# A decoder trunk on one core: the accumulators of the feed-forward block products in PSUM tiles of one bank each, and the last slab's sum in the other PSUM pool

## The chip, the cores and the metric

The kernel runs on one core of a Trainium2 chip. The metric is the device time of one execution in microseconds (us). The engines are called by the profile's names: PE is TensorE (PEld its weight loads), ACT is ScalarE, DVE is VectorE, POOL is GpSimd, SP is SyncE, which here only issues DMAs. L1395 is line 1395 of the kernel.

## The reference

One inference step of one decoder layer for 512 prompt tokens and 64 sample tokens of width 1024, in float32: a gated convolution and a gated linear recurrence side by side, a cross-attention into 256 memory tokens, and a SwiGLU feed-forward block. Only the last matters here:

```
xn = rms_norm(x, g[4])
gate, up = jnp.split(xn @ w_ffn_in, 2, axis=-1)         # 1024 -> 2 x 2816
x = x + rms_norm((jax.nn.silu(gate) * up) @ w_ffn_out, g[5])   # 2816 -> 1024
```

## The kernel before

**Products in three parts.** Every float32 matrix product is made of three matmuls on operands split into a high and a low part (high by high, high by low, low by high). The features lie on the 128 partitions and the 576 tokens (64 sample, 512 prompt) in the free dimension. A weight block is loaded to a raw tile by SP, ACT casts it to the high part (`whi`, L102) and DVE subtracts that from the raw tile to get the low part (`wlo`, L103). There are five raw buffers, four `whi` and four `wlo` buffers; blocks are prepared three ahead of their use.

**PSUM.** There are two pools of PSUM tiles. `mm` has two buffers of two banks each (`[128, 2, 512]` float32, made by `mmt`), `aux` has four buffers of one bank each (`[128, 512]`, made by `auxt`). A buffer is handed out again once all who used it are done; the tile framework adds every wait.

**The feed-forward block.** The 2816 hidden features are 22 slabs of 128. Slabs 0 to 6 are computed plainly. Slabs 7 to 21 are computed in 15 calls of `ffn_pair` (L1399): the gate and the up product of one slab, for the left and the right half of the tokens (288 each), come from seven block products instead of eight, with combinations of inputs and of weights in the manner of Strassen. Each product (`product`, L1389) is 12 matmuls of 288 columns, four blocks of features by three parts, into one accumulator. In their order the seven write accumulators 0, 1, 0, 2, 0, 1, 0. Accumulators 0 and 1 are the two banks of one `mm` tile, accumulator 2 is an `aux` tile; the three are taken at the start of the slab (`begin`, L1401). Accumulator 0 is not cleared between its four products, nor accumulator 1 between its two: a later product adds to the earlier ones. After each product one read takes what has been summed so far:

- first product, accumulator 0: `p1` (L1407), a copy on ACT; second, accumulator 1: `p5` (L1410), a copy on ACT;
- third, accumulator 0: `p6` (L1413), a copy on ACT; fourth, accumulator 2: `p2` (L1416), an add on DVE;
- fifth, accumulator 0: `p7` (L1419), on DVE; sixth, accumulator 1: `p3` (L1423), on DVE, then a silu on ACT (L1426);
- seventh, accumulator 0: `p4` (L1432, L1433), two multiplications on DVE, then the split of the result on ACT and DVE (L102, L103).

**The order.** From here on the order of PE, ACT and DVE is the order of the program (a manual schedule). A step of `run_steps` (L257) issues the product's matmuls, then the read of its accumulator, then half of a weight block's preparation (`w_part`, L191: one cast on ACT and one subtraction on DVE), then what is marked as late. One weight block of two products is 2 x 256 KB.

The 15 slabs come in two parts, of 7 and 8. After the first part the eight output slabs of the second linear layer add 7 slabs' contribution (`ffo_part`, L1532, one `mm` tile each). After the second part they add the last 8 slabs' contribution (`ffo`, L1559, one `mm` tile each), for output slabs 3 to 7 in two token groups of 320 and 256, the 320 group of all of them first.

**The last slab.** `last` (L1655) is the last step: output slab 7 for the group of 256 tokens. It sums in an `aux` tile, `ps`, 12 matmuls of half the product; then come the transposes of slab 6 (`tok_out`, L1592, an `aux` tile, copied out by ACT at L1599), three blocks of transposed output of the 320 group (`out_a` by `by_token`, L1463, an `aux` tile each, copied out by ACT at L1473 and sent by DMA), the column sums of squares (`sums_of`, L1602, an `aux` tile, L1606), the second 12 matmuls, and the norm, the transposes into `p2`, and the output. Three `out_a` blocks of the other half of the features are issued just before `last`.

Of the kernel before, what the change touches and what calls it, by code (L numbers as in the profile page):

```python
# [20 lines left out]
HN = T // 2  # L21
# [31 lines left out]
def decoder_step(  # L53
# [22 lines left out]
    def new(dt=F32, n=1):  # L76
        if n > 1:
            return [new(dt) for _ in range(n)]
        i = free_units.popleft()
        t = upool.tile([128, UNIT], dt, tag=f"u{i}", name=f"u{i}")  # L80
        owner[id(t)] = (i, t)
        return t

    def free(*ts):
        for t in ts:
            if isinstance(t, (list, tuple)):
                free(*t)
            else:
                i, _ = owner.pop(id(t))
                free_units.append(i)  # L90

    def mmt():
        return mm_p.tile([128, 2, 512], F32, tag="mm", name="mm")

    def auxt():
        return aux_p.tile([128, 512], F32, tag="aux", name="aux")
# [13 lines left out]
    def hs(h):  # L110
        return slice(HS[h], HS[h] + HW[h])
# [16 lines left out]
    def gemm(out, W, X, h, k0=0, nk=KT, first=True, last=True):  # L128
        wh, wl = W
        for k in range(nk):  # L130
            xh, xl = X(k0 + k, h)
            mm3(out, wh[:, k, :], wl[:, k, :], xh, xl, first and k == 0, last and k == nk - 1)
# [173 lines left out]
    def gain(v, k):  # L306
        return gT[:, v * 8 + k:v * 8 + k + 1]
# [1047 lines left out]
    def gg_split(j, cs, t):  # L1355
        if gg_h[j] is None:
            gg_h[j], gg_l[j] = new(F32R), new(F32R)
        split(gg_h[j][:, cs], gg_l[j][:, cs], t[:, cs])
# [28 lines left out]
    FF = {}  # L1387

    def product(W, b, ps, X, xs, first, last):  # L1389

        wh, wl = W
        xh, xl, o = X
        for i in range(4):
            k, x = 4 * b + i, 2 * i + o
            PE.matmul(ps, lhsT=wh[:, k, :], rhs=xh[x][:, xs], start=first and i == 0, stop=False, skip_group_check=True)  # L1395
            PE.matmul(ps, lhsT=wh[:, k, :], rhs=xl[x][:, xs], start=False, stop=False, skip_group_check=True)  # L1396
            PE.matmul(ps, lhsT=wl[:, k, :], rhs=xh[x][:, xs], start=False, stop=last and i == 3, skip_group_check=True)  # L1397

    def ffn_pair(j):  # L1399

        def begin():  # L1401
            ps = mmt()
            FF["b"] = ps[:, 0, :HN], ps[:, 1, :HN], auxt()[:, :HN]
            FF["t"], FF["u"] = new(), new()

        def p1():
            ACT.copy(FF["t"][:, L], FF["b"][0])  # L1407

        def p5():
            ACT.copy(FF["u"][:, L], FF["b"][1])  # L1410

        def p6():
            ACT.copy(FF["t"][:, R], FF["b"][0])  # L1413

        def p2():
            DVE.tensor_add(FF["t"][:, L], FF["t"][:, L], FF["b"][2])  # L1416

        def p7():
            DVE.scalar_tensor_tensor(FF["u"][:, L], FF["b"][0], -1.0, FF["u"][:, L], op0=ALU.mult, op1=ALU.subtract)  # L1419

        def p3():
            t = FF["t"]
            DVE.tensor_add(t[:, R], t[:, R], FF["b"][1])  # L1423

        def p3_late():
            ACT.activation(FF["t"][:, 0:T], FF["t"][:, 0:T], AF.Silu)  # L1426
            if j == KF - 1:
                free(x3n_h, x3n_l, t_h[0::2], t_l[0::2])

        def p4():  # L1430
            t, u = FF["t"], FF.pop("u")
            DVE.scalar_tensor_tensor(t[:, L], FF["b"][0], -1.0, t[:, L], op0=ALU.mult, op1=ALU.mult)  # L1432
            DVE.tensor_mul(t[:, R], t[:, R], u[:, L])  # L1433
            free(u)

        def p4_late():
            t = FF.pop("t")
            if j == KF - 1:
                free(t_h[1::2], t_l[1::2])
            gg_split(j, slice(0, T), t)  # L1440
            free(t)

        N, TT = (x3n_h, x3n_l), (t_h, t_l)
        return [("EG", (*N, 0), L, 0, True, True, (p1, None), begin), ("s1", (*TT, 0), L, 1, True, True, (p5, None), None),
                ("s2", (*TT, 1), R, 0, False, True, (p6, None), None), ("OG", (*N, 1), L, 2, True, True, (p2, None), None),
                ("s3", (*TT, 0), R, 0, False, True, (p7, None), None), ("s4", (*N, 1), R, 1, False, True, (p3, p3_late), None),
                ("OU", (*TT, 1), L, 0, False, True, (p4, p4_late), None)]

    def ffn_pairs(js):
        todo = [(j, p) for j in js for p in ffn_pair(j)]  # L1450
        for n in range(0, len(todo), 2):
            two = todo[n:n + 2]
            w = w_blocks([block(p[0], j) for j, p in two])
            for b, (j, (_, X, xs, bank, first, last, post, begin)) in enumerate(two):
                def pe(W=None, b=b, X=X, xs=xs, bank=bank, first=first, last=last, begin=begin):
                    if W is not None:
                        FF["W"] = W
                    if begin:
                        begin()
                    product(FF["W"], b, FF["b"][bank], X, xs, first, last)  # L1460
                step([w] if b == 0 else [], pe, post, prep="pair")
# [90 lines left out]
    def acc_add():  # L1552

        if "sq" in F:
            sq, s = F.pop("sq")
            DVE.tensor_add(F["acc"][:, s], F["acc"][:, s], sq[:, s])
            free(sq)
# [34 lines left out]
    def tok_out(n):  # L1592
        fg = F.pop(("fg", n))
        cs = slice((n % 4) * 128, (n % 4 + 1) * 128)
        ps = auxt()
        for i in range(2):
            PE.transpose(ps[:, i * 128:(i + 1) * 128], fg[:, i * 128:(i + 1) * 128], ident)
        for i in range(2):
            ACT.copy(ft[i][n // 4][:, cs], ps[:, i * 128:(i + 1) * 128])  # L1599
        free(fg)  # L1600

    def sums_of(cols):  # L1602

        ps = auxt()
        for i, src in enumerate(cols):
            PE.matmul(ps[:, i:i + 1], lhsT=src, rhs=ones_f[:, 0:1], start=True, stop=True)  # L1606
        return ps

    def rstd_from(o, m):

        v, y, q = (rs[:, o + k * m:o + (k + 1) * m] for k in range(3))
        ACT.activation(y, v, AF.Ln, scale=1.0 / D)
        ACT.activation(y, y, AF.Exp, scale=-0.5)
        DVE.tensor_mul(q, y, y)
        DVE.scalar_tensor_tensor(q, q, -0.5 / D, v, op0=ALU.mult, op1=ALU.mult)
        DVE.scalar_tensor_tensor(y, q, 1.5, y, op0=ALU.add, op1=ALU.mult)
        return y

    def finish(i, r):
        c0, m = htiles[1][i]  # L1620
        for d in range(2):
            t = ft[i][d]
            DVE.scalar_tensor_tensor(t[:, 0:512], t[:, 0:512], r, x2t[i][d][:, 0:512], op0=ALU.mult, op1=ALU.add)
            (nc.sync if i % 2 else nc.scalar).dma_start(
                out=tok_rows(y_sample, y_prompt, c0, m)[:, d * 512:(d + 1) * 512], in_=t[:, 0:512])
# [14 lines left out]
    def out_a(i, c4):  # L1640
        def go():
            c0, m = htiles[0][i]
            by_token(fA, 0, i, c4, nc.sync if i % 2 else nc.scalar, tok_rows(y_sample, y_prompt, c0, m))
        return go
# [10 lines left out]
    def last(W):  # L1655

        k0, nk = kgroups[2]
        ps, p2 = auxt(), auxt()
        gemm(ps[:, 0:256], W, G, 1, k0, 4, True, False)
        acc_add()  # L1660
        tok_out(6)
        for i in range(3):
            out_a(i, 1)()
        p0 = sums_of([F["acc"][:, c0:c0 + m] for c0, m in htiles[1]])
        gemm(ps[:, 0:256], [w[:, 4:, :] for w in W], G, 1, k0 + 4, 4, False, True)
        DVE.tensor_scalar(rs[:, 16:18], p0[:, 0:2], D * EPS, None, op0=ALU.add)
        fg, f1 = new(), fs[7][:, hs(1)]
        DVE.tensor_add(f1, f1, ps[:, 0:256])
        ACT.activation(fg[:, 320:576], f1, AF.Square)
        DVE.tensor_scalar(fg[:, 0:256], f1, gain(5, 7), None, op0=ALU.mult)  # L1670
        p1 = sums_of([fg[:, 320:448], fg[:, 448:576]])
        for i in range(2):
            PE.transpose(p2[:, i * 128:i * 128 + 128], fg[:, i * 128:i * 128 + 128], ident)
        DVE.tensor_add(rs[:, 20:22], rs[:, 16:18], p1[:, 0:2])
        r = rstd_from(20, 2)
        for i in range(2):
            ACT.copy(ft[i][1][:, 384:512], p2[:, i * 128:i * 128 + 128])
        for i in range(2):
            finish(i, r[:, i:i + 1])
# [64 lines left out]
```

## Time and profile before

| | |
|---|---|
| three runs | 1205.54, 1206.62, 1207.12 us; median 1206.62 |
| profiled execution | 1205.55 us, its span 1203.7 us |
| granted clock of PE, mean | 0.998 of full |
| busy share of the span | PE 96%, PEld 93%, DVE 56%, ACT 50%, POOL 12% |
| slabs 7 to 13 in `ffn_pair` | 877.8 to 977.6 us of the span |
| slabs 14 to 21 in `ffn_pair` | 1022.5 to 1136.7 us |
| HBM | 184 GB/s over the span |

The profile is one execution. Busy times add up the recorded durations of an engine's instructions. Matmuls are pipelined: one is recorded as taking 0.29 us while the next starts 0.13 us later, so the distance between starts tells what a matmul costs. Idle time before a group of instructions is given with the instruction that ended most of it.

### The profile page before, as it was taken

How to read it: one execution, taken by the hardware profiler on the slowest of the kernel's cores; microseconds unless marked ns; L12 is line 12 of the kernel's file. 1: busy time of each engine (PE TensorE's matmuls, PEld its weight loads, DVE VectorE, ACT ScalarE, POOL GpSimd, SP SyncE). 2: the span in 40 equal slices, each digit the busy share in tenths (PEclk: the TensorE clock that was granted, in tenths of full speed). 3: DMA queues.
4: the chain of work that ended last, by engine and by line, in shares of the span. 5: the costliest groups of instructions: out<-in, count | busy, mean ns of one | idle time of the engine just before them, and what ended most of it. 6: DMA issues, size and time to landing. Idle time of an engine off the chain costs nothing.

```text
span 1203.7 us, 21042 instructions
## 1 busy us (share of the span) xinstructions
PE 1150.5 (96%) x8524; PEld 1116.2 (93%) x8524; DVE 675.0 (56%) x1082; ACT 603.1 (50%) x1030; POOL 147.4 (12%) x301
## 2 busy tenths in 40 slices
PE   6999999999999999999999999999988899888896
PEld 5999999999999999999988999999987789777896
DVE  6666556642233346897677779883144543554445
ACT  5656556642122246665567777853344421444443
POOL 5433333112011010222100000000000000000000
PEclk9999999999999999999999999999999999999999
DMA  8556777467457455666755855653444433444602
GB/s 231 167 180 175 181 175 207 146 143 188 153 140 176 121 164 152 195 199 202 229 184 206 268 166 162 195 172 111 122 120 128 124 99 101 123 129 135 197 6 79
DMA packets 256859, 191.13 MB, mean 159 GB/s; under 512 B 9432, under 2 KB 241896, under 8 KB 256634
## 3 DMA queue, kind: packets, MB, share of 16 engines
q1 hardware_dynamic: 249812, 149.95, 41.8%
q0 software_dynamic: 6144, 38.50, 12.5%
q8 instruction: 67, 1.10, 0.4%
q10 hardware_dynamic: 806, 1.34, 0.3%
q14 instruction: 30, 0.25, 0.1%
HBM read 180.36 MB, written 40.85 MB: 184 GB/s over the span
## 4 chain that ended last, share of the span: by engine, by line
PE 90%; DVE 4%; ACT 3%; issue 1%; DMA 1%; POOL 0%; SPq 0%; DVEq 0%; ACTq 0%
PE mm L107 22%; PE mm L108 22%; PE mm L106 22%; PE mm L1395 5%; PE mm L1397 3%; PE mm L1396 3%; PE aux L1225 1%; PE aux L1209 1%; PE aux L106 1%; PE aux L107 1%; PE aux L108 1%; ACT u L102 1%; PE aux L1397 1%; PE aux L1396 1%; PE aux L1395 1%
## 5 line engine op out<-in xcount | busy, mean ns | idle before, releaser
L106 PE MATMUL mm<-u,whi 128*128 128x288 f32 (+2 forms) x2024 | 602.4, 298 | 0.3 <-ACT u L458 0.3
L108 PE MATMUL mm<-u,wlo 128*128 128x288 f32 (+2 forms) x2024 | 599.2, 296 | 0.5 <-POOL wlo L431 0.5
L107 PE MATMUL mm<-u,whi 128*128 128x288 f32 (+2 forms) x2024 | 598.7, 296 | 0.5 <-DVE u L103 0.5
L103 DVE TENSOR_TENSOR wlo<-wraw,whi 128x1024 fp32r<-128x1024 f32 (+2 forms) x294 | 303.9, 1035 | 238.8 <-ACT whi L102 230.1
L102 ACT CAST whi<-wraw 128x1024 fp32r<-128x1024 f32 (+2 forms) x294 | 261.0, 898 | 286.5 <-PE mm L107 217.7
L107 PEld LDWEIGHTS mm<-u,whi 128*128 128x128 f32 x2024 | 382.6, 189 | 2.1 <-DVE u L103 1.3
L106 PEld LDWEIGHTS mm<-u,whi 128*128 128x128 f32 x2024 | 382.6, 189 | 1.9 <-ACT u L458 0.9
L108 PEld LDWEIGHTS mm<-u,wlo 128*128 128x128 f32 x2024 | 382.3, 189 | 1.1 <-POOL wlo L431 0.9
L1395 PE MATMUL mm<-u,whi 128*128 128x288 f32 x360 | 112.4, 312 | 31.1 <-DVE u L1419 8.3
L1395 PEld LDWEIGHTS mm<-u,whi 128*128 128x128 f32 x360 | 67.5, 187 | 45.0 <-DVE u L1423 11.7
L1396 PE MATMUL mm<-u,whi 128*128 128x288 f32 x360 | 106.1, 295 | 0.0
L1397 PE MATMUL mm<-u,wlo 128*128 128x288 f32 x360 | 106.0, 294 | 0.0
L102 ACT CAST u<-u 128x576 fp32r<-128x576 f32 (+6 forms) x117 | 58.9, 532 | 90.8 <-DVE u L640 26.2
L103 DVE TENSOR_TENSOR u<-u,u 128x576 fp32r<-128x576 f32 (+6 forms) x117 | 65.4, 578 | 16.9 <-ACT u L102 16.7
L1397 PEld LDWEIGHTS mm<-u,wlo 128*128 128x128 f32 x360 | 67.6, 188 | 0.0
L1396 PEld LDWEIGHTS mm<-u,whi 128*128 128x128 f32 x360 | 67.6, 188 | 0.0
L103 DVE TENSOR_TENSOR u<-aux,u 128x512 fp32r<-128x512 f32 (+2 forms) x60 | 32.8, 584 | 3.6 <-ACT u L102 3.5
L1426 ACT ACTIVATE u<-u 128x576 f32<-128x576 f32 x15 | 10.3, 685 | 45.1 <-DVE u L1423 45.1
L102 ACT CAST u<-aux 128x512 fp32r<-128x512 f32 (+2 forms) x60 | 27.9, 514 | 6.7 <-DVE u L103 2.1
L106 PE MATMUL aux<-u,u 128*128 128x256 f32 (+1 forms) x96 | 27.8, 294 | 0.0
L107 PE MATMUL aux<-u,u 128*128 128x256 f32 (+1 forms) x96 | 27.6, 289 | 0.0
L108 PE MATMUL aux<-u,u 128*128 128x256 f32 (+1 forms) x96 | 27.6, 288 | 0.0
(290 smaller groups left out, 1204.6 us busy)
## 6 DMA issues: line engine op xcount, KB each, us to landing
wraw<-in_w_in_dram SPq DMA_DIRECT2D x48, 512.0 KB, 4.2
sum_s<-in_w_ffn_in_dram POOLq DMA_DIRECT2D x24, 960.0 KB, 8.2
wraw<-sum_s SPq DMA_DIRECT2D x60, 256.0 KB, 3.3
wraw<-in_w_ffn_in_dram SPq DMA_DIRECT2D x28, 512.0 KB, 3.7
wraw<-in_w_ffn_in_dram SPq DMA_DIRECT2D x45, 256.0 KB, 3.3
wraw<-in_w_mix_out_dram SPq DMA_DIRECT2D x16, 512.0 KB, 3.9
wraw<-in_w_kv_x_dram SPq DMA_DIRECT2D x16, 512.0 KB, 3.8
wraw<-in_w_q_x_dram SPq DMA_DIRECT2D x16, 512.0 KB, 3.7
```

What stands on the lines that cost most here:

```text
L102: ACT.copy(hi, src)
L103: DVE.tensor_sub(lo, src, f(hi))
L106: PE.matmul(out, lhsT=wh, rhs=xh, start=start, stop=False)
L107: PE.matmul(out, lhsT=wh, rhs=xl, start=False, stop=False)
L108: PE.matmul(out, lhsT=wl, rhs=xh, start=False, stop=stop)
L1209: PE.transpose(ps[:, d * 256 + i * 128:d * 256 + (i + 1) * 128], kr[i][:, h * 256 + d * 128:h * 256 + (d + 1) * 128], ident)
L1225: PE.matmul(ps[0:m], lhsT=t[:, k * 64:k * 64 + m], rhs=src, **kw)
L1395: PE.matmul(ps, lhsT=wh[:, k, :], rhs=xh[x][:, xs], start=first and i == 0, stop=False, skip_group_check=True)
L1396: PE.matmul(ps, lhsT=wh[:, k, :], rhs=xl[x][:, xs], start=False, stop=False, skip_group_check=True)
L1397: PE.matmul(ps, lhsT=wl[:, k, :], rhs=xh[x][:, xs], start=False, stop=last and i == 3, skip_group_check=True)
L1426: ACT.activation(FF["t"][:, 0:T], FF["t"][:, 0:T], AF.Silu)
```

## The change

The first two accumulators of `ffn_pair` become `aux` tiles of one bank each and the third becomes one bank of an `mm` tile. In `last` the sum moves from an `aux` tile to one bank of an `mm` tile, and the `aux` tile `p2` is taken later, behind the second sums of squares. No instruction is added or removed.

```diff
     def ffn_pair(j):
 
         def begin():
-            ps = mmt()
-            FF["b"] = ps[:, 0, :HN], ps[:, 1, :HN], auxt()[:, :HN]
+            FF["b"] = auxt()[:, :HN], auxt()[:, :HN], mmt()[:, 0, :HN]
             FF["t"], FF["u"] = new(), new()
...
     def last(W):
 
         k0, nk = kgroups[2]
-        ps, p2 = auxt(), auxt()
+        ps = mmt()[:, 0, :]
         gemm(ps[:, 0:256], W, G, 1, k0, 4, True, False)
...
-        p1 = sums_of([fg[:, 320:448], fg[:, 448:576]])
+        p1, p2 = sums_of([fg[:, 320:448], fg[:, 448:576]]), auxt()
```

## Rows read from the trace of the kernel before

**Rows 1.** the page: busy time, share of the span and instructions of each engine

```profile
PE 1150.5 (96%) x8524; PEld 1116.2 (93%) x8524; DVE 675.0 (56%) x1082; ACT 603.1 (50%) x1030; POOL 147.4 (12%) x301
```

**Rows 2.** page, line 1395 on PE: busy, mean ns, idle before, releaser

```profile
L1395 PE MATMUL mm<-u,whi 128*128 128x288 f32 x360 | 112.4, 312 | 31.1 <-DVE u L1419 8.3
```

**Rows 3.** line 1395: idle before it until the named instruction, us and times

```profile
...
  DVE u L1419: 20.0, 30
...
  ACT u L1410: 18.1, 30
...
```

**Rows 4.** timeline, products A to F of one pair: start, us, engine, line

```profile
907.75 0.29 PE L1397 MATMUL mm<-u,wlo 128*128 128x288 f32 x1
...
908.08 0.40 ACT L1407 COPY u<-mm 128x288 f32<-128x288 f32 x1
...
908.53 0.40 PE L1395 MATMUL mm<-u,whi 128*128 128x288 f32 x1 [0.49 <-ACT u L1407]
...
908.77 0.30 PE L1396 MATMUL mm<-u,whi 128*128 128x288 f32 x1
...
911.11 0.30 PE L1396 MATMUL mm<-u,whi 128*128 128x288 f32 x1
...
915.63 0.29 PE L1397 MATMUL mm<-u,wlo 128*128 128x288 f32 x1
915.96 0.46 DVE L1419 SCALAR_TENSOR_TENSOR u<-mm,u 128x288 f32<-128x288 f32 x1 [0.54 <-PE mm L1397]
...
916.71 0.30 PE L1396 MATMUL mm<-u,whi 128*128 128x288 f32 x1
```

**Rows 5.** chain that ended last, in order of time: start, us, engine, line

```profile
1060.72 0.47 DVE u L1419
...
1132.06 0.47 DVE u L1419
```

**Rows 6.** timeline of the same pair: reads of one tile beside writes of another

```profile
906.56 0.29 PE L1397 MATMUL mm<-u,wlo 128*128 128x288 f32 x1
906.57 0.46 DVE L1432 SCALAR_TENSOR_TENSOR u<-mm,u 128x288 f32<-128x288 f32 x1 [1.40 <-PE mm L1397]
...
912.78 0.40 ACT L1413 COPY u<-mm 128x288 f32<-128x288 f32 x1 [1.45 <-PE mm L1397]
...
914.16 0.29 PE L1395 MATMUL mm<-u,whi 128*128 128x288 f32 x1
...
918.86 0.69 ACT L1426 ACTIVATE u<-u 128x576 f32<-128x576 f32 x1 [3.49 <-DVE u L1423]
```

**Rows 7.** stretches: us, busy PE, PEld, DVE, ACT, POOL, granted clock, DMA share, GB/s

```profile
905.00:962.00 57.00, 48.70 (x338) 44.99 (x337) 29.36 (x53) 24.76 (x49) 0.00 (x0) 1.00 0.43 124
700.00:760.00 60.00, 59.96 (x452) 58.94 (x451) 52.15 (x88) 45.77 (x82) 1.62 (x3) 1.00 0.59 172
1196.00:1204.00 8.00, 0.68 (x6) 0.44 (x5) 3.38 (x8) 0.73 (x4) 0.00 (x0) 0.69 0.36 134
```

**Rows 8.** SP's waits in 880 to 1136 us; the page's DMA issues

```profile
SPq L185 <- DVE wlo L103: 169.0, 53, 5.4
...
wraw<-sum_s SPq DMA_DIRECT2D x60, 256.0 KB, 3.3
```

**Rows 9.** timeline of the last slab: start, us, engine, line

```profile
1189.17 0.39 PE L106 MATMUL aux<-u,whi 128*128 128x256 f32 x1 [0.92 <-ACT u L1599]
...
1190.21 1.07 ACT L1473 COPY u<-aux 128x512 f32<-128x512 f32 x2 [0.62 <-ACT u L1473]
1190.22 0.28 PE L108 MATMUL aux<-u,wlo 128*128 128x256 f32 x1
...
1191.73 0.43 ACT L1599 COPY u<-aux 128x128 f32<-128x128 f32 x2 [0.45 <-PE aux L1470]
...
1192.22 0.66 PE L1470 MATMUL aux<-ident,u 128*128 128x128 f32 x4 [0.23 <-ACT u L1599]
...
1192.71 0.58 PE L1606 MATMUL aux<-ones_f,u 128*128 128x1 f32 x4
```

## The prediction, made before the changed kernel was run

> **What bounds the kernel now.** I began with the page's busy shares: TensorE (PE) is busy in 96% of the span, VectorE (DVE) in 56%, ScalarE (ACT) in 50% [rows 1]. So only what PE does, or waits for, can move the time. Next come the page's groups of instructions. Nearly all of PE's lines have under 1 us of idle time before them; line 1395, the first matmul in each step of a block product, has 31.1 us, and no other line that the change touches comes near it [rows 2]. The view of that single line names the four instructions it waits for: the reads of an accumulator at lines 1407, 1410, 1419 and 1423, each 30 times (15 pairs, once on PE and once on its weight load); two of the four rows are shown, the other two read the same [rows 3].
>
> The timeline says why. Call the seven products of a pair A to G in their order: A, C, E, G write bank 0 of the `mm` tile, B and F write its bank 1, D writes the `aux` tile. A's last matmul starts at 907.75, p1 (line 1407) copies bank 0 from 908.08 for 0.40 us, and B, which writes bank 1, starts only at 908.53, when that copy is over [rows 4]. B needs nothing from the copy: its bank is another. So the wait is kept by tile and not by bank. C waits in the same way for p5's read of B's bank, F for p7's read of bank 0, G for p3's read of bank 1. At the borders where the neighbour lies in another tile nothing waits: A runs on while p4 still reads the pair before in the other `mm` buffer (906.56 beside 906.57), and E, which really needs p6's copy of bank 0 (912.78, 0.40 us), starts at 914.16 without a wait, because D stood between [rows 6].
>
> **The change, part by part.**
>
> *Removed: four waits per pair.* I measure them between starts. From the second matmul of C (911.11) to the last of E (915.63) are 34 steps without a wait: 4.52 / 34 = 0.1329 us each. From A's last matmul to B's second are 908.77 - 907.75 = 1.02 us where two steps would take 0.27: 0.75 lost; from E's last to F's second 916.71 - 915.63 = 1.08: 0.81 lost [rows 4]. With the equal ones at C and G that is 2 x 0.75 + 2 x 0.81 = 3.12 us per pair. A check by the period: the chain passes line 1419 at 1060.72 and, five pairs later, at 1132.06, so a pair takes 71.34 / 5 = 14.27 us [rows 5]; its 84 matmuls need 84 x 0.1329 = 11.16; the rest is 3.11. Over 15 pairs: 15 x 3.12 = **46.8 us**.
>
> The idle column would give less: 31.1 us [rows 2], and a sum of 1174. The two differ because a matmul is booked busy for 0.29 to 0.40 us while the next one starts 0.13 later. The Trainium skill, Trainium Kernel Development and Optimization, section Performance Expectations, says that matmul busy time is a bad metric because matmuls are pipelined; by that rule the starts are to be taken, and the trace agrees (a row of 0.29 us repeats every 0.133). I take 46.8 and leave 31.1 out of the range, since the period confirms the former.
>
> *Left in their place: the true waits.* After the change bank 0 and bank 1 are `aux` tiles of their own and the third accumulator is an `mm` tile. A write then waits only for the last read of its own bank, which always has one product or more in between: C for p1 across B, E for p6 across D, F for p5 across three products, G for p7 across F. C's first matmul is due 13 steps, 1.73 us, after A's last; p1 ends 0.33 + 0.40 = 0.73 us after it [rows 4], so 1.0 us is spare. G after p7: 0.33 + 0.46 = 0.79 against 1.73. E after p6 has that same form today and shows no wait [rows 6]. Cost: zero; if DVE or ACT were late by over 0.9 us it would come back. Behind p3 stands the silu, which must be done before p4: it runs 918.86 to 919.55 [rows 6], F's last matmul is at 916.71 + 10 x 0.133 = 918.04, so it ends 1.51 us after that one; p4 is due 1.59 + 0.33 = 1.92 after it. Covered, by 0.4 us, and nothing on PE waits for p4 in the next pair.
>
> *Moved: buffers.* `aux` has four buffers and a pair now takes two, so pairs alternate as they do on two `mm` buffers today. The third accumulator takes one `mm` buffer, freed after D. No instruction or DMA is added. The kind of tile does not change a matmul's duration: products into `aux` today keep the same step, D being inside the 34 steps above.
>
> *The other engines in a shorter pair.* The stretch 905 to 962 holds four periods: DVE 29.36 / 4 = 7.3 us per pair, ACT 24.76 / 4 = 6.2, both below 11.16. Weights: 7 blocks of 256 KB per pair are 1.835 MB; in 11.16 us that is 164 GB/s, against 124 now. The stretch 700 to 760 moved 172 GB/s with PE busy for 59.96 of its 60 us [rows 7]. SP, which issues these loads, mostly waits for a raw buffer to come free (169.0 us) and not for data, and a load lands 3.3 us after its issue [rows 8]; five raw buffers hold five times two products, some 16 us of work. Cost: zero.
>
> *The last slab.* Its accumulator leaves the `aux` ring. Today its first matmul waits 0.92 us for the copy at line 1599 to free a buffer. It loses that wait, but ACT's chain of copies and output issues sets the pace here: the fourth block of transposes waits for the copy at 1191.73 to 1192.16, and the column sums (line 1606) come only after it, 1192.71 [rows 9]. With one `aux` buffer more, those transposes go ahead of that copy, and the sums follow it directly: 1192.71 - 1192.22 = 0.49 us earlier, and with them the second half of the slab and the tail. Bounds: 0, if ACT is the whole bound, and 0.92, the whole first wait; I take **0.5**, the piece that stands on the chain.
>
> **Sum:** the profiled execution, 1205.55 us, less 46.8 and 0.5, gives 1158.3. The median shown is 1206.62, 1.07 above it; the same offset gives **1159 us**. Taking the step as 0.132 instead moves it by 1 us, the bounds of the tail by 0.5: alone this case lies in 1157 to 1162.
>
> **Rivals.**
>
> 1. *One wait per pair takes the place of the four.* If the ring handed A of the next pair the `aux` buffer that p4 still reads, A would wait as F does now, 0.81 us, in the 13 pairs that follow a pair: 10.5 us, 1169.5. Against it: A does not wait today on two buffers, and the first matmul of the last slab waited for the oldest buffer's copy, not the newest [rows 6, 9]. Chance 0.07.
> 2. *Supply catches PE.* If the loads only came half-way, 144 GB/s, a pair would take 1.835 MB / 144 = 12.74 us, 1.58 more than 11.16: 24 us back, 1183. For it: the stage's blocks come on one queue. Against: 172 GB/s elsewhere, and SP's waits [rows 7, 8]. Chance 0.05.
> 3. *Nothing changes.* The dependence could go by pool or by engine rather than by tile. Then 1206, or 0.5 less with the tail. Against it: the last slab's matmuls write an `aux` buffer (1190.22) while ACT reads other `aux` buffers (1190.21, for 1.07 us) [rows 9]. The Trainium skill, Perfetto Trace Analysis, section Optimization Strategy, reads a gap that repeats as a possible sign that there is no room to allocate the next tile; by that rule a change that adds no buffer would leave the gaps, and the time, as they are. The trace disagrees: A and D, the writers into new buffers, do not wait, while B, C, F and G write into buffers held since the pair began. Chance 0.05.
> 4. *Slower: PE runs the prepared weights dry, stands in lumps, and its clock falls.* Place: the pair stage, beyond rival 2. The clock does drop in this kernel: 0.69 on average in the last 8 us, where PE had 0.68 us of work, and 1.00 in the pair stage with its stops of under 1 us [rows 7]. At the lower level a product takes 12 x 0.133 = 1.6 us more. With rival 2's 1.58 us lost, 1.54 of the 3.12 is left, so one such product per pair decides; two make 15 x (1.58 + 3.2 - 3.12) = 25 us, 1231. Against it is all that speaks against rival 2. Chance 0.03.
>
> **How the numbers follow.** The forecast has 0.80. Its range with the working of both bounds is 1157 to 1162; I stretch it to 1156 and, to take in rival 1, to 1171. A measurement of this kernel can tell about 0.2% (2.4 us) from no change. Faster: forecast and rivals 1 and 2, 0.92; same: rival 3, 0.05; slower: rival 4, 0.03.
>
> **What would show it.** Right: line 1395 with next to no idle time on PE, 11.2 us between pairs, about 160 GB/s in the stage, clock 1.00, the sums of the last slab directly behind the copy at 1599. Wrong: line 1395 waiting for 1432 (rival 1), PE or DVE waiting for the raw weights (rival 2), the same four releasers as now (rival 3), a clock under 1.00 in the pair stage (rival 4).

## The result, and the profile after the change

The changed kernel takes 1158.35 us (median; 1157.59 to 1158.93) where the kernel before took 1206.08 us beside it. The ratio is 0.9603, with a 95% interval of 0.9587 to 0.9620. The forecast was 1159, the range 1156 to 1171.

The profiled execution took 1157.59 us, its span is 1155.8 us, 47.9 less than before, with the same mean clock of 0.998. The page's busy shares and its group for line 1395, which answer to [rows 1] and [rows 2]:

```profile
PE 1134.3 (98%) x8524; PEld 1113.9 (96%) x8524; DVE 675.0 (58%) x1082; ACT 603.2 (52%) x1030; POOL 146.9 (13%) x301
...
L1395 PE MATMUL aux<-u,whi 128*128 128x288 f32 x360 | 105.9, 294 | 0.0
```

DVE and ACT do the same work as before to 0.1 us. Line 1395 has no idle time left, against 31.1 us. PE's busy time *fell*, by 16.2 us, though it executes the same matmuls. The page's busy time of an engine counts time in which matmuls overlap only once; 8524 matmuls of 0.29 us, added up, would be more than twice the span. (The busy time of a group, as in the second line, is the sum of its durations.) Before the change the first matmul after each of the 60 stops lay alone for 0.24 us until the next one began (908.53 to 908.77 in [rows 4]) instead of 0.13, and the last one before the stop lay alone for all of its 0.29 us instead of 0.13: (0.11 + 0.16) x 60 = 16.2. Idle time and this time together, 31.1 + 16.2 = 47.3, are what starts against starts had shown.

The changed file is one line shorter behind the edit, so that p1 is now L1406, p5 L1409, p6 L1412, p2 L1415, p7 L1418, p3 L1422, the silu L1425 and p4 L1431. The timeline of the end of A, the start of B, and the end of E up to p4 in one pair, answering to [rows 4] (start, us, engine, line):

```profile
901.23 0.29 PE L1397 MATMUL aux<-u,wlo 128*128 128x288 f32 x1
...
901.36 0.30 PE L1395 MATMUL aux<-u,whi 128*128 128x288 f32 x1
...
901.56 0.40 ACT L1406 COPY u<-aux 128x288 f32<-128x288 f32 x1
...
907.59 0.30 PE L1397 MATMUL aux<-u,wlo 128*128 128x288 f32 x1
907.72 0.29 PE L1395 MATMUL aux<-u,whi 128*128 128x288 f32 x1
...
907.92 0.46 DVE L1418 SCALAR_TENSOR_TENSOR u<-aux,u 128x288 f32<-128x288 f32 x1 [0.55 <-PE aux L1397]
...
909.19 0.30 PE L1397 MATMUL aux<-u,wlo 128*128 128x288 f32 x1
909.33 0.29 PE L1395 MATMUL aux<-u,whi 128*128 128x288 f32 x1
...
910.01 0.69 ACT L1425 ACTIVATE u<-u 128x576 f32<-128x576 f32 x1 [2.68 <-DVE u L1422]
...
910.77 0.29 PE L1397 MATMUL aux<-u,wlo 128*128 128x288 f32 x1
...
911.17 0.46 DVE L1431 SCALAR_TENSOR_TENSOR u<-aux,u 128x288 f32<-128x288 f32 x1 [0.59 <-PE aux L1397]
```

B starts 0.13 us after A's last matmul and runs while p1 copies accumulator 0 (901.56 to 901.96). F starts 0.13 us after E's last matmul and overlaps p7, and G follows F without a step missed, 1.74 us after E's last matmul; p7 had ended at 908.38. The period, from p4 to p4 four pairs later, answering to [rows 5]:

```profile
900.05 0.46 DVE L1431 SCALAR_TENSOR_TENSOR u<-aux,u 128x288 f32<-128x288 f32 x1 [0.59 <-PE aux L1397]
...
944.53 0.46 DVE L1431 SCALAR_TENSOR_TENSOR u<-aux,u 128x288 f32<-128x288 f32 x1 [0.59 <-PE aux L1397]
```

44.48 / 4 = 11.12 us a pair, against 14.27; over 84 matmuls that is 0.1324 us each, no step lost. Busy time of four periods, answering to [rows 7] (columns as there):

```profile
905.00:949.50 44.50, 44.50 (x338) 44.50 (x337) 28.76 (x51) 24.33 (x48) 0.00 (x0) 1.00 0.54 157
```

And SP's waits in 880 to 1090 us, answering to [rows 8] (us in total, times, longest):

```profile
SPq L185 <- DVE wlo L103: 136.3, 53, 5.4
```

PE is busy for the whole stretch, at clock 1.00, with loads of 157 GB/s. SP still spends 136.3 us waiting for raw buffers to come free, and PE waits for no load.

The last slab, answering to [rows 9]. The last addition of the residual before the change (line 1636 there, 1635 now):

```profile
1188.72 0.83 DVE L1636 TENSOR_TENSOR u<-u,u 128x640 f32<-128x640 f32 x1
```

And the slab after the change:

```profile
1140.60 0.36 PE L106 MATMUL mm<-u,whi 128*128 128x256 f32 x1
...
1141.31 0.83 DVE L1635 TENSOR_TENSOR u<-u,u 128x640 f32<-128x640 f32 x1
...
1144.33 0.43 ACT L1598 COPY u<-aux 128x128 f32<-128x128 f32 x2 [0.45 <-PE aux L1469]
...
1144.81 0.61 PE L1605 MATMUL aux<-ones_f,u 128*128 128x1 f32 x4 [0.23 <-ACT u L1598]
```

The first matmul waits for nothing (0.92 us before). The column sums stand directly behind ACT's copy, 3.50 us after the last addition of the residual began on DVE (L1635); before the change the same distance was 3.99 (1188.72 to 1192.71): 0.49 gained.

### The profile page after: what moved, and what is told of

Its sections match the earlier page's. It is cut to its first block, busy times and chain, and to the rows that moved or that the text cites. A ratio compares the mean times of both kernels' runs of the same rounds, so it can differ in the third digit from the quotient of the medians.

```text
span 1155.8 us, 21040 instructions
## 1 busy us (share of the span) xinstructions
PE 1134.3 (98%) x8524; PEld 1113.9 (96%) x8524; DVE 675.0 (58%) x1082; ACT 603.2 (52%) x1030; POOL 146.9 (13%) x301
## 4 chain that ended last, share of the span: by engine, by line
PE 94%; DVE 2%; ACT 1%; DMA 1%; issue 1%; POOL 0%; SPq 0%; DVEq 0%; ACTq 0%
PE mm L107 23%; PE mm L108 23%; PE mm L106 23%; PE aux L1397 4%; PE aux L1396 4%; PE aux L1395 4%; PE aux L1225 1%; PE aux L1209 1%; PE aux L106 1%; PE aux L107 1%; PE aux L108 1%; PE mm L1397 1%; PE mm L1396 1%; PE mm L1395 1%; DMA wraw<-in_w_in_dram 1%
## 5 line engine op out<-in xcount | busy, mean ns | idle before, releaser
L107 PEld LDWEIGHTS mm<-u,whi 128*128 128x128 f32 x2032 | 384.5, 189 | 2.4 <-DVE u L103 1.3
L106 PEld LDWEIGHTS mm<-u,whi 128*128 128x128 f32 x2032 | 384.3, 189 | 2.2 <-ACT u L458 1.2
L108 PEld LDWEIGHTS mm<-u,wlo 128*128 128x128 f32 x2032 | 384.0, 189 | 0.8 <-POOL wlo L431 0.6
L1397 PE MATMUL aux<-u,wlo 128*128 128x288 f32 x360 | 106.2, 295 | 0.0
L1396 PE MATMUL aux<-u,whi 128*128 128x288 f32 x360 | 106.1, 295 | 0.0
L1395 PE MATMUL aux<-u,whi 128*128 128x288 f32 x360 | 105.9, 294 | 0.0
L1397 PEld LDWEIGHTS aux<-u,wlo 128*128 128x128 f32 x360 | 67.6, 188 | 0.0
L1395 PEld LDWEIGHTS aux<-u,whi 128*128 128x128 f32 x360 | 67.6, 188 | 0.0
L1396 PEld LDWEIGHTS aux<-u,whi 128*128 128x128 f32 x360 | 67.6, 188 | 0.0
L1425 ACT ACTIVATE u<-u 128x576 f32<-128x576 f32 x15 | 10.3, 686 | 32.9 <-DVE u L1422 32.9
```

Source lines behind the costliest of these rows:

```text
L106: PE.matmul(out, lhsT=wh, rhs=xh, start=start, stop=False)
L107: PE.matmul(out, lhsT=wh, rhs=xl, start=False, stop=False)
L108: PE.matmul(out, lhsT=wl, rhs=xh, start=False, stop=stop)
```

## The experiments

**One part of the change at a time.** The accumulators of `ffn_pair` alone:

```diff
-            ps = mmt()
-            FF["b"] = ps[:, 0, :HN], ps[:, 1, :HN], auxt()[:, :HN]
+            FF["b"] = auxt()[:, :HN], auxt()[:, :HN], mmt()[:, 0, :HN]
```

> Only the accumulators of ffn_pair are changed; the last slab keeps its aux tile. Theory (four waits per pair, 0.75 to 0.81 us each, kept by tile): all of the 46.8 us of the pair stage, so about 1158.8 us, 0.5 over the changed kernel; line 1395 without idle time; the first matmul of the last slab waits 0.9 us as before. Rival (the stage's gain needs the freed aux buffer of the last slab too, or the tail is a larger part): over 1160 us.

Measured: 1158.68 us (ratio 0.9605, 0.9591 to 0.9620), line 1395 without idle time. The last slab keeps its wait of 0.92 us, as expected, and its sums start 4.01 us behind L1635. And the last slab alone (`ps = mmt()[:, 0, :]`, `p2` taken late):

> Only the sum of the last slab is moved; ffn_pair as before. Theory: about 0.5 us less than the kernel before, 1205.6 us, hardly to be told from no change in time; in the profile the column sums of the last slab start 0.5 us earlier against the last DVE addition of line 1636 than before (3.99 us behind its start before). Rival (ACT is the whole bound there): 0.0 us.

Measured: 1205.74 us against 1206.03, ratio 0.9993 (0.9983 to 1.0003). In time that is no difference that can be told; its trace shows the mechanism:

```profile
1189.89 0.82 DVE L1636 TENSOR_TENSOR u<-u,u 128x640 f32<-128x640 f32 x1
...
1193.40 0.61 PE L1606 MATMUL aux<-ones_f,u 128*128 128x1 f32 x4 [0.23 <-ACT u L1599]
```

3.51 us, 0.48 less than before. So the pair stage has all of the gain but half a microsecond.

**Which accumulators share a tile.** The order of the products is 0, 1, 0, 2, 0, 1, 0. In the changed kernel no two share. First another assignment in which none does:

```diff
-            FF["b"] = auxt()[:, :HN], auxt()[:, :HN], mmt()[:, 0, :HN]
+            FF["b"] = mmt()[:, 0, :HN], auxt()[:, :HN], auxt()[:, :HN]
```

> Accumulator 0 in an mm tile of its own (the second bank unused), accumulators 1 and 2 in aux tiles. Theory (what counts is that neighbours in the order lie in different tiles, not which pool or how many banks a tile has): the same time as the changed kernel, 1158.3 us, line 1395 without idle time. Rival (the two-bank pool is what waits, or the aux pool is quicker): a share of the 47 us comes back, at least 10 us.

Measured: 1158.22 us (0.9601, 0.9586 to 0.9615), no idle time on line 1395: neither the pool nor the size of the tile matters. Then two that share without being neighbours:

```diff
-            FF["b"] = auxt()[:, :HN], auxt()[:, :HN], mmt()[:, 0, :HN]
+            ps = mmt()
+            FF["b"] = auxt()[:, :HN], ps[:, 0, :HN], ps[:, 1, :HN]
```

> Accumulators 1 and 2 are the two banks of one mm tile, accumulator 0 an aux tile. In the order 0 1 0 2 0 1 0 a product of another tile always stands between the two that share. Theory: a shared tile costs nothing then, since the false wait (of the product on 2 for the read of 1, of the second product on 1 for the read of 2) is hidden behind the product between: 1158.3 us. Rival (sharing a tile costs by itself): two false waits per pair of 0.75 to 0.81 us, 15 x 1.56 = 23 us, 1181 us.

Measured: 1157.82 us (0.9597, 0.9583 to 0.9612), again no idle time. A shared tile costs nothing by itself. Then two that share and are neighbours at two borders, third to fourth and fourth to fifth:

```diff
-            FF["b"] = auxt()[:, :HN], auxt()[:, :HN], mmt()[:, 0, :HN]
+            ps = mmt()
+            FF["b"] = ps[:, 0, :HN], auxt()[:, :HN], ps[:, 1, :HN]
```

> Accumulators 0 and 2 are the two banks of one mm tile, accumulator 1 an aux tile. In the order 0 1 0 2 0 1 0 the third, fourth and fifth products are neighbours in the shared tile, all the others are not. Theory: two waits per pair come back, the fourth product for the copy at p6 (0.75 us) and the fifth for the addition at p2 (0.81 us): 15 x 1.56 = 23.4 us, 1181.7 us; no wait for p1, p5, p7, p3. Rival (the four waits hang together, or come from accumulator 0 being shared with anything): 1158 or 1205 us.

Measured: 1181.76 us (0.9798, 0.9783 to 0.9813), 23.4 us over the changed kernel, as expected; that it fits to the tenth is luck, since the interval is 1.8 us to either side. The view of line 1395, idle time before it by what ended it, and its timeline (this file has the line numbers of the kernel before):

```profile
  DVE u L1416: 19.9, 30
  ACT u L1413: 18.1, 30
```

```profile
908.61 0.40 ACT L1413 COPY u<-mm 128x288 f32<-128x288 f32 x1 [0.68 <-PE mm L1397]
...
909.06 0.40 PE L1395 MATMUL mm<-u,whi 128*128 128x288 f32 x1 [0.49 <-ACT u L1413]
...
910.94 0.46 DVE L1416 TENSOR_TENSOR u<-u,mm 128x288 f32<-128x288 f32 x1 [0.69 <-PE mm L1397]
...
911.45 0.40 PE L1395 MATMUL mm<-u,whi 128*128 128x288 f32 x1 [0.55 <-DVE u L1416]
```

Both waits are back, one per border, and none for p1, p5, p7 and p3. So the waits do not hang together: each belongs to one border of neighbours in one tile. That a matmul on one bank waits for a read of the other bank of its tile, and for nothing in another tile, is shown by these three kernels with the changed one.

**How much cover a true wait has.** Additional DVE reads of accumulator 0 beside p7, which the seventh product has to wait for:

```diff
             DVE.scalar_tensor_tensor(FF["u"][:, L], FF["b"][0], -1.0, FF["u"][:, L], op0=ALU.mult, op1=ALU.subtract)
+            for _ in range(2):
+                DVE.scalar_tensor_tensor(FF["u"][:, R], FF["b"][0], -1.0, FF["t"][:, R], op0=ALU.mult, op1=ALU.subtract)
```

> The changed kernel with two more DVE reads of accumulator 0 beside p7, into an unused part of a scratch tile. The last matmul of the fifth product and the first of the seventh are 13 steps, 1.73 us, apart; p7 ends 0.79 us after the former, each further read adds 0.38 us, so the third ends at 1.55 us. Theory: covered, no wait, 1158.3 us. Rival (the spare time is less than worked out, since DVE has other work in the way): a wait of up to 0.5 us per pair, 7 us.

Measured: 1159.60 us (two executions; 0.9614, 0.9595 to 0.9633), 1.25 over the changed kernel, 0.08 per pair. The intervals overlap, but the timeline below shows the same 0.08. And with four:

> As the one with two further reads, with four: the last ends 0.79 + 4 x 0.38 = 2.31 us after the fifth product's last matmul, 0.58 us beyond the 1.73. Theory: the seventh product waits for it, 0.58 and 0.1 of restart in each of 15 pairs, 10 us, 1168.5 us; line 1395 waits on DVE for the added read. Rival (the cover is longer than worked out): 1158 us.

Measured: 1174.44 us (two executions; 0.9737, 0.9718 to 0.9757), 16.1 over the changed kernel, 1.07 per pair. The timelines of both, from E's last matmul to G's first (line 1420 is that of the added reads), two and then four:

```profile
908.66 0.29 PE L1397 MATMUL aux<-u,wlo 128*128 128x288 f32 x1
...
909.37 0.94 DVE L1420 SCALAR_TENSOR_TENSOR u<-aux,u 128x288 f32<-128x288 f32 x2
...
910.39 0.37 PE L1395 MATMUL aux<-u,whi 128*128 128x288 f32 x1
...
910.60 0.30 PE L1396 MATMUL aux<-u,whi 128*128 128x288 f32 x1
```

```profile
910.74 0.29 PE L1397 MATMUL aux<-u,wlo 128*128 128x288 f32 x1
...
911.44 1.93 DVE L1420 SCALAR_TENSOR_TENSOR u<-aux,u 128x288 f32<-128x288 f32 x4
...
913.42 0.40 PE L1395 MATMUL aux<-u,whi 128*128 128x288 f32 x1 [0.79 <-DVE u L1420]
```

The size of a read was wrong in both expectations, the limit was not. The added reads follow each other at 0.48 us, not 0.38; they all write the same place, which may be why, but no run separates that. Two end at 910.31, 1.65 us after E's last matmul, and G's second matmul comes 0.21 instead of 0.13 us after its first: the very edge. Four end at 913.37, 2.63 us after it; G starts 2.68 after, where it is due at 1.73, which is 0.95, and with 0.1 of restart about the 1.07 of a pair. So a read is covered if it ends a little less than 1.65 us after the start of the last matmul before it; the real p7 ends after 0.79.

**Is a second set of buffers needed?** The ground of rival 1 of the prediction, no second set of buffers, built with `mm` tiles:

```diff
-            FF["b"] = auxt()[:, :HN], auxt()[:, :HN], mmt()[:, 0, :HN]
+            FF["b"] = mmt()[:, 0, :HN], mmt()[:, 0, :HN], auxt()[:, :HN]
```

> Accumulators 0 and 1 take one mm tile each, so a pair uses up both mm buffers and has no second set; accumulator 2 is an aux tile. Theory: the four false waits are gone, and one true one is new per pair: the first product waits for p4's read of the pair before, 0.81 us, in 13 pairs, and the first step of the plain products behind each part may wait the same: 15 x 0.81 = 12 us, 1170.5 us; line 1395 waits for line 1431 alone. Rival (the number of buffers is what the change gained by): far more, near 1200 us.

Measured: 1159.12 us (0.9606, 0.9590 to 0.9622), and no idle time on line 1395: a miss. A pair uses up both `mm` buffers, and still the next one does not wait. My explanation was the order in which buffers come free, which the next kernel was to turn round:

```diff
-            FF["b"] = mmt()[:, 0, :HN], mmt()[:, 0, :HN], auxt()[:, :HN]
+            b1, b0 = mmt()[:, 0, :HN], mmt()[:, 0, :HN]
+            FF["b"] = b0, b1, auxt()[:, :HN]
```

> As the kernel with accumulators 0 and 1 in one mm tile each, but the tile of accumulator 1 is asked for first and that of accumulator 0 second. Theory (a buffer freed earlier is handed out earlier: in that kernel the next pair's first product got the buffer freed by p3 in the sixth step, and the second product the one freed by p4, a product later, so nothing waited): now accumulator 0 gets the buffer that p4 still reads, the first product of a pair waits for it, 0.81 us, in 13 to 15 pairs, 11 to 12 us, 1169.5 us, and line 1395 waits for p4 alone. Rival (buffers go by first use, or the second set is not needed at all): 1158.5 us.

Measured: 1159.29 us (0.9617, 0.9601 to 0.9633), no wait either. The timeline at the border of two pairs in it, from the first matmul of the next pair's A on (this file too has the line numbers of the kernel before):

```profile
912.08 0.29 PE L1395 MATMUL mm<-u,whi 128*128 128x288 f32 x1
...
912.35 0.29 PE L1397 MATMUL mm<-u,wlo 128*128 128x288 f32 x1
912.35 0.46 DVE L1432 SCALAR_TENSOR_TENSOR u<-mm,u 128x288 f32<-128x288 f32 x1 [0.59 <-PE mm L1397]
912.48 0.29 PE L1395 MATMUL mm<-u,whi 128*128 128x288 f32 x1
```

The next pair's matmuls start at 912.08 and run on while p4 reads an `mm` tile (912.35 to 912.81). With two buffers in all, they must write the one that p3 read a product earlier, whichever tile was asked for first. That a buffer is bound at a tile's first use, and not where it is asked for, would give this; it fits both kernels but no run isolates it. Shown is the price: no wait, and no difference in time that can be told (the intervals overlap that of the changed kernel). The second set of buffers gains nothing here: one accumulator of a pair is free a product before the other, and the next pair can begin in it.

**Does the supply of weights have room?** `bufs=5` of the raw weight tiles to `bufs=3`:

> The changed kernel with three raw weight buffers in place of five. Three hold 3 x 3.19 = 9.6 us of the pair stage's work; a load lands 3.3 us after its issue and a buffer is held some 3 us by the cast and the subtraction. Theory (supply has room in the pair stage): no idle time on line 1395 and 11.2 us per pair also with three; the total may rise through other stages, whose blocks are 512 KB. Rival (supply is just enough and the prefetch depth carries it): the pair stage shows waits for the raw tiles, a longer period than 11.2 us, and the time rises by over 5 us there.

Measured: 1177.93 us (0.9768, 0.9752 to 0.9784), 19.6 over the changed kernel. In the pair stage nothing of it:

```profile
897.90 0.29 PE L1395 MATMUL aux<-u,whi 128*128 128x288 f32 x1
...
1110.23 0.46 DVE L1431 SCALAR_TENSOR_TENSOR u<-aux,u 128x288 f32<-128x288 f32 x1 [0.59 <-PE aux L1397]
```

From the first product to the last p4 that is 212.33 us; in the changed kernel it runs from 877.54 to 1089.53, 211.99. All but 0.3 us of the loss lies before the stage, which starts 20.4 us later; there the chain now goes through loads of weights, above all of the cached values between 638 and 663 us. SP's waits for raw buffers in the stage come to 135.1 us here, as good as the 136.3 with five, so their sum does not tell how much room the supply has; that line 1395 has no idle time does. So at 11.12 us a pair the supply does not even need the five buffers that it has.

**The tail.** In the last 15 us PE still stands at several places. Two tries: first all `out_a` blocks of the first half issued by SP (`nc.sync if i % 2 or c4 == 0 else nc.scalar`), then all six by SP, and the three of the second half moved behind the norm's copies. In the first try the edit moves the three blocks of the first half alone; the "six" of its expectation is a slip:

> The changed kernel with all six output blocks of the first half of the features in the 320 group issued by SP in place of ACT, which issues two of the three now. In the changed kernel ACT spends 0.55 and 0.38 us on these issues just before the copy at line 1598 that the column sums wait for. Theory (ACT's chain sets the pace of the tail): that copy comes 0.9 us earlier and the time falls by 0.5 to 0.9 us, to 1157.6. Rival (DVE's additions or PE set it by then): 0.0 to 0.2 us.

Measured: 1157.19 us (1156.20 to 1158.26; ratio 0.9590, 0.9574 to 0.9606). The squares of the last slab start 4.92 us behind the last addition (L1635) instead of 6.13, 1.2 earlier, more than expected; the time is 1.2 below that of the changed kernel, but the intervals overlap, so a gain is likely and not settled.

> The changed kernel with the six output blocks of the 320 group issued by SP, and the three blocks of the second half of the features transposed, copied and sent only behind the norm's copies in the last slab, so that the second half of the slab's matmuls does not stand behind them. Theory (in the tail PE's second half of the slab stands behind transposes that wait for ACT's copies): the squares of the last slab start some 2 us earlier against the last DVE addition of line 1635 than in the changed kernel (6.1 us behind its start there), and the time falls by 1 to 2 us, to 1156.8. Rival (the late output blocks then end last, or delay the final DMAs on ACT): no gain, or up to 1 us more.

Measured: 1158.59 us (0.9609, 0.9595 to 0.9624). The squares start 3.91 us behind L1635, 2.2 earlier, as the theory had it, and the time does not fall, as the rival had it. From its timeline, the last addition, the squares, and the last work:

```profile
1141.67 0.83 DVE L1635 TENSOR_TENSOR u<-u,u 128x640 f32<-128x640 f32 x1
...
1145.58 0.42 ACT L1666 ACTIVATE u<-u 128x256 f32<-128x256 f32 x1 [1.76 <-DVE u L1665]
...
1147.95 2.74 DVE L1622 SCALAR_TENSOR_TENSOR u<-u,rs,u 128x512 f32<-128x512 f32 x4
...
1150.06 1.82 SPq L1623 DMA_DIRECT2D out_dram<-u  x2
```

And the rate in its DMA view, in 40 slices of 1140 to 1156 us:

```profile
GB/s 0 0 20 0 0 0 0 0 0 148 174 333 379 358 241 5 0 0 0 0 0 0 0 164 164 287 379 410 399 399 399 389 394 389 394 92 0 0 0 0
```

The late blocks and the last slab's outputs leave together: for nine slices, 3.6 us up to 1154, DMA runs at 379 to 410 GB/s, where the changed kernel's mean over its span is 165. In the changed kernel the last outputs leave alone, 1.05 MB in the last burst at up to 396 GB/s; here the burst is 1.70 MB (both estimated from the rates and the slices). From L1635 to the end of the span it is 14.13 us here and 14.49 in the changed kernel, so of the 2.2 us some 0.4 are left in the tail of this profile. That the late blocks hold up the last outputs fits this, but no run separates it.

## Why the prediction was right

**Four waits, 46.8 us.** Right. From the first product to the last p4 the stage took 259.15 us before (877.78 to 1136.93) and 211.99 after: 47.16 gained. The step came out at 0.1324 us, against the 0.1329 used. The choice to go by starts and not by the idle column (31.1) decided the number: by the column the forecast would have been 1174, 16 us off. The offset from the profile to the median, taken as 1.07 us, is 0.53 over the four executions of the kernel before and 0.76 in the changed one; from profile to profile the gain was 47.96, against 47.3 forecast.

**The cause.** Right, and shown, not only argued: the wait follows the tile (the three assignments), one border at a time, at 0.75 and 0.81 us.

**True waits covered.** Right. p1 and p7 keep about 0.8 us to spare; the limit, worked out as 1.73 us, was found a little under 1.65 by the added reads. The silu ends 1.51 us after F's last matmul, as worked out (909.19 to 910.70). p4 begins 0.40 us after G's last matmul, not 0.33, which leaves 0.47 us between the silu and p4.

**Other engines and supply.** Right: DVE 7.2 and ACT 6.1 us a pair (28.76 and 24.33 over four), 157 GB/s where 164 had been worked out, and room even with three raw buffers.

**The last slab, 0.5 us.** Right in size and place: 0.48 alone and 0.49 in the changed kernel, with the sums directly behind the copy. ACT's chain is the bound there: with ACT's two issues given to SP, the copy that the sums wait for came 1.72 us behind L1635 instead of 3.02, and the sums 2.38 instead of 3.50.

**The sum.** 47.16 and 0.49 make 47.65 of the 47.9 us between the spans; the remaining 0.25 is the start of the pair stage, 877.78 against 877.54, ahead of anything that changed.

**The rivals.** None came true. Rival 1 did not come true even on ground that should have favoured it: with `mm` tiles and no second set no wait appears. Rival 2 fell with the run on three raw buffers, and rival 4 with it; the clock stayed at 1.00 in the stage. Rival 3, dependence by pool or by engine, is refuted by the neighbours in `aux` tiles that run without a wait.

## What to carry to other kernels

If PE stops for a fraction of a microsecond at the border of two accumulations, look whether the accumulator just finished and the next one lie in one tile: here a tile of two banks made each bank wait for reads of the other, and separate tiles, or an order in which neighbours never share, took away all of it. Price such stops by the distance between starts and by the period, since idle time alone missed a third of the cost. Before adding buffers, work out which read frees each of them: staggered ends can do the work of a second set.

## What had not been expected

Two buffers in all for accumulators 0 and 1 show no wait that two sets would save (1159.1 and 1159.3 against 1158.35 us). Added DVE reads of one accumulator that write to one place follow each other at 0.48 us, not at the 0.38 us seen between others. And moving work off PE's and ACT's way in the tail, which brought the squares 2.2 us forward, gave no time that could be told in the runs; more output was then left for the end.
